# Diagonal inverses in a half-width tile copied by ScalarE, two key fetches moved back, and other ranks for the woven jobs

## The chip, the cores and the metric

One core of one Trainium2 chip. The metric is the device time of one execution in microseconds (us); each run gives one such time. The engines are TensorE (PE in the profile; PEld are its weight loads), VectorE (DVE), ScalarE (ACT), GpSimd (POOL) and SyncE (SP), whose queue issues every DMA of this kernel.

## The reference, cut to what matters

A decoder step of two layers over 1024 prompt tokens and 8 x 4 sample tokens, width 1024. Layer 0 is sliding-window attention (16 query heads on 4 key heads), in which the sample tokens also see 128 cached keys and values. Layer 1 is gated DeltaNet: 16 value heads on 8 key heads, in chunks of 64 tokens, each of which needs the inverse of a unit lower triangular matrix.

```
def swa_sample_core(q, k, v, k_buf, v_buf, sinks):
    k_all = jnp.concatenate([k_buf.astype(k.dtype), k], axis=1)
...
    p = sink_softmax(logits, mask, sinks)
...
def gated_delta_chunked(q, k, v, g, beta, s0, chunk):
...
    lower = jnp.where(strict, jnp.einsum('nbhik,nbhjk->nbhij', kb, kc) * decay, 0.0)
    rhs = jnp.concatenate([vc * bc[..., None], kb * jnp.exp(gc)[..., None]], axis=-1)
    sol = lax.linalg.triangular_solve(lower + jnp.eye(chunk, dtype=lower.dtype), rhs,
                                      left_side=True, lower=True, unit_diagonal=True)
...
    def step(S, xs):
        w_v_c, w_k_c, qk_c, q_dec_c, k_dec_c, g_tot_c = xs
        u = w_v_c - jnp.einsum('bhck,bhkv->bhcv', w_k_c, S)
        o = jnp.einsum('bhck,bhkv->bhcv', q_dec_c, S) + jnp.einsum('bhij,bhjv->bhiv', qk_c, u)
        S = S * g_tot_c[..., None, None] + jnp.einsum('bhck,bhcv->bhkv', k_dec_c, u)
        return S, o
```

## The kernel before

Every projection runs on TensorE in split precision: weights and activations are cut into a high and a low part (`wh` and `wl`, `hhi` and `hlo`), and each of the 8 steps over the 1024 inputs is three matmuls, high by high, low by high and high by low. The tokens are taken in three groups of 384, 384 and 288 columns. The kernel is one chain of such projection matmuls; everything else is a set of Python generators, the jobs, whose instructions are put between them.

The order is fixed while the program is built. Between two projection matmuls `stages()` goes through the jobs in the order of their ranks (`K` by name of job, `KT` for the closing, `KR` by DeltaNet round) and lets each run that is not held back. A job holds itself with `ready` (its tile is done by a planner's clock), `soon` and `idle` (done, or its engine free, within a margin: `AM` in the layers, `AT` in the closing), or waits for a PSUM `bank`. The planner (`class Core`) gives each issued instruction a cost and a due time. So a new number in these tables, or another cost, moves instructions of all engines from there to the end; each engine then runs its own list strictly in order.

The stages, by time in the profile: a head written out by hand (0 to 50 us); attention (50 to 390), near whose end `cached` treats the sample tokens in four pairs; the projection `wo` back to the model width (390 to 500); DeltaNet in 8 rounds, one for each key head (500 to 1340); the output projection of DeltaNet, woven with the last rounds' state chain and the sample states (the closing, 1340 to 1590); a tail.

`cached` fetches for each pair `KT` and `vc` from the caches by `cached_rows` and a mask `smk`. `cached_pair` scores them into a PSUM bank (`kxs,qz` and `KT,qz`), takes the softmax on VectorE and ScalarE (`sp`, `smx`, `snm`, `es`, `ssu`), turns it on TensorE (`erl,sp`; `erl` holds the identity) and multiplies by the values (`spT,vc`). `load_wo` fetches the weights of `wo` (`wor`, `wr`), ScalarE rounds them to `whi`, and VectorE or GpSimd, by `GP[0]`, takes the rest `wlo`.

In a DeltaNet round `solve` builds the triangular matrices `UZ` and stores their 32 x 32 diagonal blocks in DRAM (`Ld`). `invert` loads them as `X`, 64 blocks at a time on 2 x 64 partitions, and solves for the inverse with 31 pairs of VectorE operations; it stores the result to `Xdd` and loads it back turned, as `Xc`. `diagonal` writes `Xc` into the block-diagonal tile `Xd`, which TensorE multiplies with `UZ` (`Xd,UZ`), and `blocks` combines the pieces (`UZ,M`). `chain` is the recurrence over the chunks: `S,kT` gives `vo`, `vo,UZ` gives `uo` (copied by ScalarE), `uo,ks` updates the state `S` on VectorE, and `S,qT` and `uo,DP` give the output.

Nearly all operations are recorded at the helper's line L84 (L83 after the change), so that the tiles tell them apart.

Of the kernel before, what the change touches and what calls it, by code (L numbers as in the profile page):

```python
# [5 lines left out]
F32 = mybir.dt.float32  # L6
# [25 lines left out]
def constants():  # L32
# [29 lines left out]
    blocks["fold32"] = (i[:, None] % 32 == np.arange(32)[None, :]) * 1.0  # L62
    order = ["ident", "fold32", "iu", "ones", "mku", "lo32", "bsel", "fold64", "wmask", "smask", "selp", "sels"]
    blocks = {k: blocks[k] for k in order}
# [29 lines left out]
class Core:  # L94
# [15 lines left out]
    def issued(self, eng, op, ins, args, kwargs):  # L110
# [18 lines left out]
        if "dma" in op:  # L129
# [168 lines left out]
def body(tc, I, O, cst_ap, dbg=None):  # L298
# [19 lines left out]
    SP = (2, 20)  # L318
    AM = (3, 12)
    AT = (-5, 3)  # L320
    EX = (1.2, 1.6, 0, 0.9)
    ES, EN, EL, EM = EX
    K = {'split': 12, 'add': 26, 'attend': 22, 'turning': 24, 'modulate': 20, 'cached': 8, 'wo': 60, 'turn': 0, 'ahead': 2, 'taps': 2, 'gating': 6, 'decay': 23, 'samples': 28, 'load': 6, 'mod': 1, 'shape': 27, 'decays': 35, 'prepare': 61, 'gather': 23, 'finish': 37, 'states': 7, 'core': 16, 'new': 8}
    KT = {'prepare': 3, 'gather': 15, 'finish': 25, 'states': 10, 'core': 7, 'new': 9, 'load': 12, 'gating': 5, 'samples': 30, 'output': 24}
    KR = [{'chain': 4, 'output': 20, 'solve': 6, 'invert': 19, 'blocks': 31, 'decayed': 22}, {'chain': 31, 'output': 29, 'solve': 13, 'invert': 31, 'blocks': 39, 'decayed': 38}, {'chain': 31, 'output': 2, 'solve': 30, 'invert': 41, 'blocks': 2, 'decayed': 6}, {'chain': 35, 'output': 37, 'solve': 4, 'invert': 4, 'blocks': 10, 'decayed': 23}, {'chain': 14, 'output': 0, 'solve': 23, 'invert': 44, 'blocks': 1, 'decayed': 57}, {'chain': 41, 'output': 36, 'solve': 8, 'invert': 4, 'blocks': 58, 'decayed': 16}, {'chain': 8, 'output': 15, 'solve': 8, 'invert': 12, 'blocks': 57, 'decayed': 12}, {'chain': 10, 'output': 18, 'solve': 42, 'invert': 34, 'blocks': 0, 'decayed': 60}]
    TB = (3, 5)
    SW = (16, 13)
    MS = (50, 5)
# [3 lines left out]
    MM = (11, 12)  # L332
    ORDER = [("q", 2), ("q", 3), ("q", 4), ("q", 5), ("z", 0), ("k", 1), ("z", 1), ("z", 2), ("q", 6), ("q", 7),
# [242 lines left out]
    def ready(*ts):  # L576
        return lambda: plain() or nc.ready(ts) <= nc.free["tensor"]
# [433 lines left out]
    if True:  # L1011
# [869 lines left out]
    if True:  # L1881
# [155 lines left out]
        def solve(hq, st):  # L2037
# [21 lines left out]
            Ld = dr.tile([64, 32, 32], F32, name="Ld", tag="Ld", bufs=2)  # L2059
            Xdd = dr.tile([2, 64, 32, 32], F32, name="Xdd", tag="Xdd", bufs=2)  # L2060
            UZ = st["UZ"] = []
# [25 lines left out]
        def invert(hq, st, Ld, Xdd):  # L2087
# [6 lines left out]
            for p in range(2):  # L2094
                nc.sync.dma_start(X[64 * p:64 * p + 64], Ld)
            yield soon(X)
            for p in range(2):
                nc.gpsimd.memset(X[64 * p:64 * p + 64].rearrange("p i c -> p (i c)")[:, 32 * p:1024:65], 1.0)
            nc.gpsimd.memset(X[64:P, 0, 0:1], 0.0)
            yield soon(X)  # L2100
            for k in range(31):
                n, m = 31 - k, k // 2 + 1
                tv = tmp[:, 0:n * m].rearrange("p (i c) -> p i c", c=m)
                yield idle("vector")
                nc.vector.tensor_tensor(tv, X[:, k, k + 1:].unsqueeze(2).to_broadcast([P, n, m]),
                                        X[:, k, 0:m].unsqueeze(1).to_broadcast([P, n, m]), ALU.mult)
                nc.vector.tensor_tensor(X[:, k + 1:, 0:m], X[:, k + 1:, 0:m], tv, ALU.subtract)
            nc.sync.dma_start(Xdd.rearrange("p q i c -> (p q) i c"), X)
            inverted[0] += 1
            yield lambda: solved[0] == hq  # L2110
            Xc = gs.tile([P, 16, 2, 16], F32, tag="Xc", name="Xc")
            for b in range(4):
                for p in range(2):
                    nc.sync.dma_start(Xc[32 * b:32 * b + 32, :, p, :],
                                      Xdd[p, 16 * b:16 * b + 16, :, 0:16].rearrange("q i c -> i q c"))

            lg, Ms, uzs = "lg", [], [t_.rearrange("p h c i -> p (h c) i") for t_ in UZ]

            def diagonal():

                for cp_, uz in enumerate(uzs):
                    xd = Xd[cp_ % 2]
                    yield soon(Xc)
                    for b in range(4):
                        bs = slice(32 * b, 32 * b + 32)
                        nc.gpsimd.tensor_tensor(xd[bs, :, bs].rearrange("i q (c p) -> i q p c", p=2), Xc[bs, 4 * cp_:4 * cp_ + 4],
                                                C["lo32"][bs, :].rearrange("i (p c) -> i p c", p=2).unsqueeze(1)
                                                .to_broadcast([32, 4, 2, 16]), ALU.mult)
                    yield lambda: st.get("pairs", 0) >= cp_ - 2
                    yield ready(xd)  # L2130
# [933 lines left out]
```

## Time and profile before

| | |
|---|---|
| time, median of 3 runs | 1600.68 us (1599.53 to 1602.54) |
| the profiled execution's own time | 1600.59 us |
| its span | 1598.8 us |
| its mean granted TensorE clock | 0.997 |
| TensorE busy | 1573.9 us, 98% |
| VectorE busy | 1215.9 us, 76% |
| ScalarE busy | 843.0 us, 53% |
| GpSimd busy | 145.1 us, 9% |

The span is the time from the first to the last instruction that the profiler records; 1.8 us of the execution's time lie outside it. Busy shares are means over stages.

### The profile page before, as it was taken

How to read it: one execution, taken by the hardware profiler on the slowest of the kernel's cores; microseconds unless marked ns; L12 is line 12 of the kernel's file. 1: busy time of each engine (PE TensorE's matmuls, PEld its weight loads, DVE VectorE, ACT ScalarE, POOL GpSimd, SP SyncE). 2: the span in 40 equal slices, each digit the busy share in tenths (PEclk: the TensorE clock that was granted, in tenths of full speed). 3: DMA queues.
4: the chain of work that ended last, by engine and by line, in shares of the span. 5: the costliest groups of instructions: out<-in, count | busy, mean ns of one | idle time of the engine just before them, and what ended most of it. 6: DMA issues, size and time to landing. Idle time of an engine off the chain costs nothing. (4 is left out here: it accounts for less than half of the span.)

```text
span 1598.8 us, 30691 instructions
## 1 busy us (share of the span) xinstructions
PE 1573.9 (98%) x10714; PEld 1404.9 (88%) x10714; DVE 1215.9 (76%) x3830; ACT 843.0 (53%) x2422; POOL 145.1 (9%) x231
## 2 busy tenths in 40 slices
PE   9999999999999999999999999999999999999997
PEld 6888888988778999999999999999999998767776
DVE  5737667676676678987988778888688887858787
ACT  4635655554344665565564655755557565523332
POOL 1300000000001002020020100202001002121121
PEclk9999999999999999999999999999999999999999
DMA  9542220106252333143433325323243136685874
GB/s 366 157 142 80 80 82 27 40 25 194 89 171 87 90 95 76 55 124 88 120 73 86 100 56 131 86 56 110 75 117 92 49 92 217 204 270 184 272 278 162
DMA packets 178572, 195.71 MB, mean 122 GB/s; under 512 B 76593, under 2 KB 120465, under 8 KB 178385
## 3 DMA queue, kind: packets, MB, share of 16 engines
q1 hardware_dynamic: 178416, 193.75, 40.0%
q8 instruction: 85, 1.39, 0.4%
q14 instruction: 71, 0.57, 0.1%
HBM read 146.45 MB, written 49.27 MB: 122 GB/s over the span
## 5 line engine op out<-in xcount | busy, mean ns | idle before, releaser
L84 PE MATMUL ps_pj<-h2hi,wh 128*128 128x384 f32 (+1 forms) x1128 | 378.1, 335 | 0.0
L84 PE MATMUL ps_pj<-h2hi,wl 128*128 128x384 f32 (+1 forms) x1128 | 377.1, 334 | 0.2 <-DVE wl L84 0.2
L84 PE MATMUL ps_pj<-h2lo,wh 128*128 128x384 f32 (+1 forms) x1128 | 376.9, 334 | 0.0
L84 PEld LDWEIGHTS ps_pj<-h2hi,wl 128*128 128x128 f32 x1128 | 213.1, 189 | 2.4 <-DVE wl L84 0.5
L84 PEld LDWEIGHTS ps_pj<-h2lo,wh 128*128 128x128 f32 x1128 | 213.3, 189 | 2.2
L84 PEld LDWEIGHTS ps_pj<-h2hi,wh 128*128 128x128 f32 x1128 | 213.2, 189 | 2.0
L84 PE MATMUL ps_pj<-hhi,wh 128*128 128x384 f32 (+1 forms) x376 | 123.8, 332 | 0.5 <-ACT hhi L84 0.4
L84 PE MATMUL ps_pj<-hlo,wh 128*128 128x384 f32 (+1 forms) x376 | 122.8, 330 | 0.0
L84 PE MATMUL ps_pj<-hhi,wl 128*128 128x384 f32 (+1 forms) x376 | 122.3, 329 | 0.0
L84 POOL TENSOR_TENSOR Xd<-Xc,cst 32x128 f32<-32x128 f32 x128 | 67.1, 524 | 456.5 <-DMA Xc<-Xdd 307.2
L84 DVE SCALAR_TENSOR_TENSOR vT<-XR,cT,vT 128x384 f32<-128x384 f32 (+1 forms) x144 | 82.6, 579 | 16.8 <-ACT vT L84 15.0
L84 DVE TENSOR_TENSOR wl<-wr,wh 128x512 fp32r<-128x512 f32 x120 | 82.9, 691 | 10.6 <-ACT wh L84 9.9
L84 ACT CAST wh<-wr 128x512 fp32r<-128x512 f32 x128 | 78.6, 616 | 18.7 <-PE ps_pj L84 17.9
L84 PEld LDWEIGHTS ps_pj<-hlo,wh 128*128 128x128 f32 x376 | 70.6, 188 | 8.2 <-issue 7.7
L84 PEld LDWEIGHTS ps_pj<-hhi,wh 128*128 128x128 f32 x376 | 70.5, 188 | 6.6 <-issue 4.8
L84 ACT COPY XR<-ps_pj 128x384 f32<-128x384 f32 (+1 forms) x96 | 43.6, 454 | 57.4 <-PE ps_pj L84 57.0
L84 PEld LDWEIGHTS ps_pj<-hhi,wl 128*128 128x128 f32 x376 | 70.6, 188 | 3.7 <-issue 3.7
L84 ACT ACTIVATE prob<-prob,nm 128x256 f32<-128x256 f32 (+1 forms) x128 | 62.3, 489 | 18.9 <-DVE nm L84 18.8
L84 DVE TENSOR_TENSOR X<-X,tmp 128x126 f32<-128x126 f32 (+22 forms) x248 | 63.8, 257 | 8.5
L84 DVE TENSOR_TENSOR tmp<-X 128x126 f32<-128x126 f32 (+22 forms) x248 | 62.4, 252 | 8.2 <-POOL X L84 3.6
L84 ACT ACTIVATE qe<-ps_mi,Eg 128x128 f32<-128x128 f32 x112 | 35.0, 364 | 63.0 <-PE ps_mi L84 59.8
L84 POOL TENSOR_TENSOR xt<-xt,y 128x512 f32<-128x512 f32 x30 | 42.5, 1419 | 182.9 <-DVE y L84 166.9
(555 smaller groups left out, 3824.5 us busy)
## 6 DMA issues: line engine op xcount, KB each, us to landing
wr<-in_gwb SPq DMA_DIRECT2D x96, 256.0 KB
S<-in_states SPq DMA_DIRECT2D x42, 256.0 KB
wm<-in_wm SPq DMA_DIRECT2D x16, 512.0 KB
wr<-in_winb SPq DMA_DIRECT2D x32, 256.0 KB
wmod<-in_w_mod SPq DMA_DIRECT2D x32, 256.0 KB
wm<-in_w_mod SPq DMA_DIRECT2D x32, 256.0 KB
DP<-gcr SPq DMA_DIRECT2D x64, 128.0 KB
zl<-zd SPq DMA_DIRECT2D x32, 256.0 KB
```

The lines of the kernel that those rows point to most:

```text
L84: inst = fn(*args, **kwargs)
```

## The change

It has six parts.

1. `invert` solves into a clean tile `Y` of 16 columns, which GpSimd clears and gives its unit diagonal, where the inverse was written over the lower half of `X`; `Xdd` has half the size.
2. In `diagonal`, `Xd` is written by 128 ScalarE copies where it was 128 GpSimd multiplications with the mask `lo32`. The copies wait for `idle("scalar", Xc)` each, and the wait for `pairs` stands ahead of them.
3. `cached_pair` fetches pairs 2 and 3 only when the pair before has its keys (`looked`).
4. `gct` lies in another pool, and the unread output of `turn_sum` is one shared tile `jk`.
5. The planner takes a load to 64 partitions as 0.8 longer.
6. `GP[0]` is 1: the second half of each of the 8 rows of `wlo` goes to GpSimd. The other tables get new numbers, of which a few lines stand below (`EX`, `KT`, `KR`, `TB`, `SW`, `MS` and `MM` change in the same manner).

```diff
@@ -132,6 +131,8 @@
             self.moved = max(start + 0.7, self.moved) + 2.4 * size + 0.0005 * rows
             end = self.moved + self.dl[0 if outs[0].space == DRAM else 1]
+            if outs[0].space != DRAM and outs[0].shape[0] == 64:
+                end += 0.8
...
@@ -316,20 +317,20 @@
-    AM = (3, 12)
-    AT = (-5, 3)
+    AM = (2, 14)
+    AT = (-6, 7)
...
-    GP = (0, 0, 0, 0, 1)
-    ORD = ['zzkv', 'zqvzk', 'zqzkv', 'qzzvk', 'qzzkv', 'vqzzk', 'qzzkv', 'qvzz']
+    GP = (1, 0, 0, 0, 1)
+    ORD = ['zzkv', 'zqvzk', 'zqvzk', 'zqzkv', 'qzzkv', 'vqzzk', 'qzzkv', 'qvzz']
...
@@ -1326,10 +1327,11 @@
-            yield lambda: paired[0] >= b2 - 2
+            yield lambda: paired[0] >= b2 - 2 and (b2 < 2 or looked[0] >= b2 - 1)
             KT, vc = held[b2] if b2 < 2 else cached_rows(b2)
             yield lambda: paired[0] >= b2 - 1
             yield ready(KT)
+            looked[0] += 1
...
@@ -2093,26 +2096,26 @@
-            yield soon(X)
+            Y = gs.tile([P, 32, 16], F32, tag="Y", name="Y")
+            nc.gpsimd.memset(Y, 0.0)
             for p in range(2):
-                nc.gpsimd.memset(X[64 * p:64 * p + 64].rearrange("p i c -> p (i c)")[:, 32 * p:1024:65], 1.0)
-            nc.gpsimd.memset(X[64:P, 0, 0:1], 0.0)
-            yield soon(X)
+                nc.gpsimd.memset(Y[64 * p:64 * p + 64].rearrange("p i c -> p (i c)")[:, 16 * p:512:33], 1.0)
+            yield soon(X, Y)
...
-                                        X[:, k, 0:m].unsqueeze(1).to_broadcast([P, n, m]), ALU.mult)
-                nc.vector.tensor_tensor(X[:, k + 1:, 0:m], X[:, k + 1:, 0:m], tv, ALU.subtract)
-            nc.sync.dma_start(Xdd.rearrange("p q i c -> (p q) i c"), X)
+                                        Y[:, k, 0:m].unsqueeze(1).to_broadcast([P, n, m]), ALU.mult)
+                nc.vector.tensor_tensor(Y[:, k + 1:, 0:m], Y[:, k + 1:, 0:m], tv, ALU.subtract)
+            nc.sync.dma_start(Xdd.rearrange("p q i c -> (p q) i c"), Y)
...
@@ -2120,13 +2123,11 @@
-                    yield soon(Xc)
+                    yield lambda: st.get("pairs", 0) >= cp_ - 2
                     for b in range(4):
                         bs = slice(32 * b, 32 * b + 32)
-                        nc.gpsimd.tensor_tensor(xd[bs, :, bs].rearrange("i q (c p) -> i q p c", p=2), Xc[bs, 4 * cp_:4 * cp_ + 4],
-                                                C["lo32"][bs, :].rearrange("i (p c) -> i p c", p=2).unsqueeze(1)
-                                                .to_broadcast([32, 4, 2, 16]), ALU.mult)
-                    yield lambda: st.get("pairs", 0) >= cp_ - 2
+                        yield idle("scalar", Xc)
+                        nc.scalar.copy(xd[bs, :, bs].rearrange("i q (c p) -> i q p c", p=2), Xc[bs, 4 * cp_:4 * cp_ + 4])
```

What this moves is seen in the lists of the engines, of which three places stand here. The number of built matmuls is the same before and after, 9022; the groups in which they are not projection matmuls are 560 before and 555 after.

**The cached pairs.** TensorE, end of the attention layer, before; `...` stands for projection matmuls (`ps_pj`) alone:

```order
L84 MATMUL ps_lg<-kxs,qz 32x32 x8
L84 MATMUL ps_lg<-KT,qz 32x128 x8
L84 MATMUL ps_pj<-hlo,wh 128x384
...
L84 MATMUL ps_lg<-kxs,qz 32x32 x8
L84 MATMUL ps_lg<-KT,qz 32x128 x8
...
L84 MATMUL ps_pj<-hhi,wh 128x288
L84 MATMUL ps_mi<-erl,sp 128x128
L84 MATMUL ps_mi<-erl,sp 32x128
```

and after the change:

```order
L83 MATMUL ps_lg<-kxs,qz 32x32 x8
L83 MATMUL ps_lg<-KT,qz 32x128 x8
...
L83 MATMUL ps_lg<-kxs,qz 32x32 x8
L83 MATMUL ps_lg<-KT,qz 32x128 x8
...
L83 MATMUL ps_mi<-erl,sp 128x128
L83 MATMUL ps_mi<-erl,sp 32x128
L83 MATMUL ps_pj<-hlo,wh 128x384
L83 MATMUL ps_mi<-erl,sp 128x128
L83 MATMUL ps_mi<-erl,sp 32x128
L83 MATMUL ps_pj<-hhi,wl 128x384
```

Before, 21 projection matmuls (5 of 288 columns, 16 of 384) stand between the last attention block's `ob<-pT,vsb` and the first of these groups, 5 between the two groups, and 28 from the second group to the first `erl,sp`; the second pair's `erl,sp` comes far behind. After, they are 26 (18 of 288, 8 of 384), 6 and 14, and the second pair's `erl,sp` follows one matmul behind the first's.

SP's queue at that place, before and then after; `in_wob` are the weights of `wo`:

```order
L84 DMA wr<-in_wob 128x512 x2
L84 DMA KT<-in_keysT 64x1024
L84 DMA vc<-in_cache_swa_v 128x2x256
...
L84 DMA smk<-in_cst 128x640
L84 DMA KT<-in_keysT 64x1024
L84 DMA vc<-in_cache_swa_v 128x2x256
L84 DMA wor<-in_wob 128x512 x4
```

```order
L83 DMA wr<-in_wob 128x512
L83 DMA KT<-in_keysT 64x1024
L83 DMA vc<-in_cache_swa_v 128x2x256
...
L83 DMA smk<-in_cst 128x640
L83 DMA wor<-in_wob 128x512 x3
L83 DMA KT<-in_keysT 64x1024
L83 DMA vc<-in_cache_swa_v 128x2x256
```

One `wr` fewer stands ahead of the first keys, and the third pair's keys stand behind three `wor`. VectorE runs, before, the first softmax through to its end and then the second; after, both are interleaved: `sp`, `smx`, `snm`, `es` of the one and of the other, then the two sums and divisions.

**GpSimd's list**, from the `wo` weights to the second DeltaNet round, before:

```order
L84 MEMSET spT 128x128 x4
L84 TENSOR_TENSOR kw0l<-wr,kw0h 128x512
...
L84 MEMSET X 64x16 x2
L84 MEMSET X 64x1
L84 TENSOR_TENSOR Xd_6460<-Xc,cst 32x4x2x16 x4
L84 TENSOR_TENSOR Xd_6462<-Xc,cst 32x4x2x16 x4
```

and after:

```order
L83 TENSOR_TENSOR wlo<-wor,whi 128x512
L83 MEMSET spT 128x128 x2
L83 TENSOR_TENSOR wlo<-wor,whi 128x512 x3
...
L83 TENSOR_TENSOR wlo<-wr,whi 128x512 x4
L83 TENSOR_TENSOR kw0l<-wr,kw0h 128x512
...
L83 MEMSET Y 128x512
L83 MEMSET Y 64x16 x2
```

Eight subtractions `wlo` have come to GpSimd, and in each of the 8 rounds 16 multiplications into `Xd` have gone, for one full and two strided memsets of `Y`; ScalarE's list has 16 copies into `Xd` more in each round.

**The state chain of the last round**, on TensorE in the closing, before:

```order
L84 MATMUL ps_pj<-h2lo,ohi 128x512
L84 MATMUL ps_ob<-vo,UZ 128x128 x2
L84 MATMUL ps_mi<-uo,ks 128x128 x2
L84 MATMUL ps_mi<-S,qT 128x256
L84 MATMUL ps_mi<-uo,DP 128x128 x2
L84 MATMUL ps_pj<-h2hi,ohi 128x512
```

and the tightest place after:

```order
L83 MATMUL ps_mi<-uo,ks 128x128 x2
L83 MATMUL ps_mi<-S,qT 128x256
L83 MATMUL ps_mi<-uo,DP 128x128 x2
L83 MATMUL ps_mi<-S,kT 128x256
L83 MATMUL ps_tr<-erl,vo 128x128 x8
L83 MATMUL ps_ob<-vo,UZ 128x128 x2
L83 MATMUL ps_pj<-h2hi,ohi 128x512
L83 MATMUL ps_pj<-h2hi,of 128x512
L83 MATMUL ps_mi<-uo,ks 128x128 x2
```

Before, `uo,ks` follows `vo,UZ` with nothing between them at one place and with one matmul at another; after, at least two projection matmuls stand between them everywhere. In turn `S,kT` now follows `uo,DP` at once at one place, with `erl,vo` alone between it and `vo,UZ`.

## Rows read from the trace of the kernel before

**Rows 1.** The page: span, and busy time of each engine.

```profile
span 1598.8 us, 30691 instructions
PE 1573.9 (98%) x10714; PEld 1404.9 (88%) x10714; DVE 1215.9 (76%) x3830; ACT 843.0 (53%) x2422; POOL 145.1 (9%) x231
```

**Rows 2.** Windows: stretch, us, busy PE, PEld, DVE, ACT, POOL; clock, DMA share, GB/s.

```profile
357.00:370.00 13.00, 11.80 (x123) 10.70 (x123) 4.47 (x18) 3.00 (x9) 0.35 (x2) 1.00 0.96 257
500.00:1340.00 840.00, 837.28 (x6107) 804.41 (x6106) 688.06 (x2182) 496.33 (x1461) 74.65 (x161) 1.00 0.34 90
1340.00:1500.00 160.00, 153.51 (x812) 112.65 (x811) 120.04 (x323) 66.58 (x163) 23.30 (x21) 1.00 0.73 231
```

**Rows 3.** Waits of TensorE, 1340 to 1500: releaser, total, times, longest.

```profile
PE ps_pj L84 <- DVE y L84: 1.1, 1, 1.1
...
PE ps_mi L84 <- DVE S L84: 0.7, 1, 0.7
```

**Rows 4.** Timeline of TensorE: start, duration, operation; an attention visit.

```profile
348.41 0.34 PE L84 MATMUL ps_pj<-hhi,wl 128*128 128x384 f32 x1
348.58 0.34 PE L84 MATMUL ps_pj<-hhi,wh 128*128 128x384 f32 x1
348.76 1.04 PE L84 MATMUL ps_mi<-erl,prob 128*128 128x128 f32 x8
349.55 0.42 PE L84 MATMUL ps_pj<-hlo,wh 128*128 128x384 f32 x1
```

**Rows 5.** Timeline of the cached pairs, all engines; in brackets the idle time before.

```profile
340.73 15.86 SPq L84 DMA_DIRECT2D wr<-in_wob  x2
...
361.93 0.64 PE L84 MATMUL ps_lg<-KT,qz 64*32 64x128 f32 x16 [1.16 <-DMA vc<-in_cache_swa_v]
...
365.91 0.32 DVE L84 CUSTOM_DVE_ANT_0 sp<-ps_lg,smk 128x160 f32<-128x160 f32 x1 [6.16 <-DMA smk<-in_cst]
...
368.15 0.56 DVE L84 SCALAR_TENSOR_TENSOR zo<-th,zo 128x384 f32<-128x384 f32 x1
...
369.01 0.30 DVE L84 TENSOR_SCALAR sp<-sp,ssu 128x160 f32<-128x160 f32 x1
...
369.49 0.38 PE L84 MATMUL ps_mi<-erl,sp 128*128 128x128 f32 x2
```

**Rows 6.** Timeline of the closing's state chain; then the group of all `olo`.

```profile
1354.81 0.71 PE L84 MATMUL ps_mi<-uo,ks 128*128 128x128 f32 x4 [0.52 <-ACT uo L84]
...
1361.18 1.28 POOL L84 TENSOR_TENSOR xt<-xt,y 128x512 f32<-128x512 f32 x1 [15.85 <-DVE y L84]
1361.22 1.79 DVE L84 TENSOR_TENSOR olo<-of,ohi 128x512 fp32r<-128x512 f32 x1
...
1365.63 0.67 PE L84 MATMUL ps_mi<-S,kT 128*128 128x256 f32 x2 [0.70 <-DVE S L84]
L84 DVE TENSOR_TENSOR olo<-of,ohi 128x512 fp32r<-128x512 f32 x30 | 22.5, 754 | 15.2 <-ACT ohi L84 15.0
```

**Rows 7.** By tile `Xd`: durations in ns, min/median/max; GpSimd's waits; then two ScalarE groups.

```profile
L84 POOL TENSOR_TENSOR Xd<-Xc,cst x128: 442/455/1004, 624.3 to 1328.0; 32x128 f32<-32x128 f32 x128
L84 POOL MEMSET Xd<- x2: 528/528/529, 549.8 to 550.2; 128x512 f32 x2
...
  DMA Xc<-Xdd: 307.2, 24
...
L84 ACT ACTIVATE vo<-vo,fo 128x128 f32<-128x128 f32 x128 | 41.5, 394 | 9.9 <-DVE fo L84 9.9
L84 ACT ACTIVATE jk<-ps_lg 128x128 f32<-128x128 f32 x120 | 33.5, 279 | 14.5 <-PE ps_lg L84 11.8
```

**Rows 8.** Timeline: last `wlo` on VectorE, its use on TensorE, a GpSimd subtraction.

```profile
395.26 1.90 DVE L84 TENSOR_TENSOR wlo<-wr,whi 128x512 fp32r<-128x512 f32 x3 [1.14 <-ACT whi L84]
...
401.50 0.39 PE L84 MATMUL ps_mi<-wlo,ohi 128*128 128x512 f32 x1
...
493.97 1.36 POOL L84 TENSOR_TENSOR kw0l<-wr,kw0h 128x512 fp32r<-128x512 f32 x1 [116.37 <-DMA xt<-in_x_prompt]
```

More of the change, by code (lines that the diff above doesn't have):

```diff
@@ L62, in constants @@
     blocks["fold32"] = (i[:, None] % 32 == np.arange(32)[None, :]) * 1.0
-    order = ["ident", "fold32", "iu", "ones", "mku", "lo32", "bsel", "fold64", "wmask", "smask", "selp", "sels"]
+    order = ["ident", "fold32", "iu", "ones", "mku", "bsel", "fold64", "wmask", "smask", "selp", "sels"]
     blocks = {k: blocks[k] for k in order}
@@ L318, in body @@
     SP = (2, 20)
-    AM = (3, 12)
-    AT = (-5, 3)
-    EX = (1.2, 1.6, 0, 0.9)
+    AM = (2, 14)
+    AT = (-6, 7)
+    EX = (0.7, 1.6, 0, 0.9)
     ES, EN, EL, EM = EX
-    K = {'split': 12, 'add': 26, 'attend': 22, 'turning': 24, 'modulate': 20, 'cached': 8, 'wo': 60, 'turn': 0, 'ahead': 2, 'taps': 2, 'gating': 6, 'decay': 23, 'samples': 28, 'load': 6, 'mod': 1, 'shape': 27, 'decays': 35, 'prepare': 61, 'gather': 23, 'finish': 37, 'states': 7, 'core': 16, 'new': 8}
-    KT = {'prepare': 3, 'gather': 15, 'finish': 25, 'states': 10, 'core': 7, 'new': 9, 'load': 12, 'gating': 5, 'samples': 30, 'output': 24}
@@ L326, in body @@
-    TB = (3, 5)
-    SW = (16, 13)
-    MS = (50, 5)
+    K = {'split': 16, 'add': 11, 'attend': 22, 'turning': 24, 'modulate': 5, 'cached': 33, 'wo': 60, 'turn': 0, 'ahead': 2, 'taps': 2, 'gating': 6, 'decay': 22, 'samples': 52, 'load': 6, 'mod': 1, 'shape': 27, 'decays': 35, 'prepare': 31, 'gather': 40, 'finish': 58, 'states': 4, 'core': 1, 'new': 37}
+    KT = {'prepare': 3, 'gather': 35, 'finish': 38, 'states': 10, 'core': 7, 'new': 11, 'load': 12, 'gating': 5, 'samples': 37, 'output': 32}
@@ L329, in body @@
+    TB = (3, 6)
+    SW = (1, 22)
+    MS = (51, 9)
     AH, AI = (a / 10 for a in AM)
-    GP = (0, 0, 0, 0, 1)
-    ORD = ['zzkv', 'zqvzk', 'zqzkv', 'qzzvk', 'qzzkv', 'vqzzk', 'qzzkv', 'qvzz']
-    MM = (11, 12)
+    GP = (1, 0, 0, 0, 1)
+    ORD = ['zzkv', 'zqvzk', 'zqvzk', 'zqzkv', 'qzzkv', 'vqzzk', 'qzzkv', 'qvzz']
+    MM = (11, 18)
     ORDER = [("q", 2), ("q", 3), ("q", 4), ("q", 5), ("z", 0), ("k", 1), ("z", 1), ("z", 2), ("q", 6), ("q", 7),
@@ L1834, in decays @@
         yield soon(p2)
+        gct = ab.tile([P, P], F32, name="gct")
         nc.scalar.copy(gct, p2[:, 0:P])
@@ L1858, in decays @@
             nc.gpsimd.memset(Xd[i], 0.0)
+        junk.append(gs.tile([P, P], F32, name="jk"))
         weave(decay_blocks(0, states[0]), "decay")
@@ L2023, in turn_sum @@
                     nc.tensor.transpose(pt[:, c * P:(c + 1) * P], src[:, cc * P:(cc + 1) * P], ident)
-                jk = gs.tile([P, P], F32, tag="jk" if ktok is None else "jn", name="jk")
+                jk = junk[0]
                 for c in range(4):
@@ L2059, in solve @@
             Ld = dr.tile([64, 32, 32], F32, name="Ld", tag="Ld", bufs=2)
-            Xdd = dr.tile([2, 64, 32, 32], F32, name="Xdd", tag="Xdd", bufs=2)
+            Xdd = dr.tile([2, 64, 32, 16], F32, name="Xdd", tag="Xdd", bufs=2)
             UZ = st["UZ"] = []
@@ L2114, in invert @@
                     nc.sync.dma_start(Xc[32 * b:32 * b + 32, :, p, :],
-                                      Xdd[p, 16 * b:16 * b + 16, :, 0:16].rearrange("q i c -> i q c"))
+                                      Xdd[p, 16 * b:16 * b + 16].rearrange("q i c -> i q c"))
             lg, Ms, uzs = "lg", [], [t_.rearrange("p h c i -> p (h c) i") for t_ in UZ]
```

6 lines of the change are left out of this document (2 added, 4 removed).

## The prediction

> **What bounds the kernel now.** The page comes first [rows 1]: TensorE is busy for 1573.9 of 1598.8 us, VectorE for 76%, ScalarE for 53%, GpSimd for 9%. So time can be gained only where TensorE stands still, 24.9 us in all, or by fewer or cheaper matmuls. The windows by stage come next, since a mean over stages hides where that is [rows 2]: in DeltaNet, 840 us long, TensorE lacks 840 - 837.28 = 2.7 us; in the closing 160 - 153.51 = 6.5 us; in the 13 us around the cached pairs 1.2 us. That is 10.4 of the 24.9; the rest is the head, which the change leaves alone, and the tail behind the last matmul. The waits of TensorE in the closing are several of about a microsecond, each with a releaser of its own (the residual sum `y` 1.1, the state `S` 0.7) [rows 3]. The granted clock is 1.00 in all these windows, so there is none to win. The reader is to see: whatever work the change takes from GpSimd, VectorE or ScalarE counts only as far as it shortens one of these waits. The sum is made against the profiled execution's 1600.59 us, 0.09 below the median of the runs.
>
> **Matmuls and their groups.** The built matmuls are as many as before. Five groups of other matmuls between the projection ones are gone. What a visit costs beyond its own matmuls is seen at one in attention [rows 4]: projection matmuls start 0.17 us apart, and the first behind the visit takes 0.42 in place of 0.34, so 0.08. Five fewer give -0.4; the ends are 0, if the visit costs nothing, and -0.8, at twice the row.
>
> **The cached pairs.** Now TensorE waits 1.16 us for the first pair's loads, at 361.93, and reaches the first `erl,sp` at 369.49, just behind the division that ended at 369.01 + 0.30 = 369.31 [rows 5]. That softmax began at 365.91, when the mask `smk` landed (6.16 us idle, released by its DMA), and took 3.4 us, of which VectorE spent the time up to 368.71 on other work, `zo` last.
>
> After the change, 26 projection matmuls stand ahead of the first keys' scores where 21 did. At 0.174 us for 384 columns and, in proportion, 0.13 for 288, that is 8 x 0.174 + 18 x 0.13 = 3.7 us against 16 x 0.174 + 5 x 0.13 = 3.4: TensorE arrives 0.3 later, so the wait for loads is 0.85 if they land as now. From there to the first `erl,sp` stand 6 + 14 = 20 matmuls where 5 + 28 = 33 did, 13 x 0.174 = 2.3 us less: TensorE gets there at about 367.2 on the clock of now. The softmax is shorter too, since nothing but the second pair's first half lies in it: from 3.4 us take off `th` and `zo`, 2 x 0.56 = 1.1, leaving 2.3, so 365.9 + 2.3 = 368.2. If `smk` lands as now, TensorE waits 1.0 us there and about 0.2 at the second pair, one matmul later: 0.85 + 1.2 = 2.05 against 1.16, a loss of 0.9. But one `wr` of 256 KB fewer stands ahead in the queue, whose stage moves 257 GB/s at a DMA share of 0.96 [rows 2]; that is 1.0 us. If all lands so much earlier, the wait for the loads is gone and the one for `sp` is about 0.9 in all (the start moves ahead with the loads): a gain of 0.3. I take the middle, +0.3. The ends: -1.2, if nothing is left of any wait, and +3, if the softmax takes its 3.4 us as now and the second pair adds 0.7. Pairs 2 and 3 are fetched later, behind three or six `wor`; their scores come some 20 matmuls (3.5 us) or more behind, and the row's DMA share says that the queue is full, so that is part of the +3.
>
> **The closing.** `uo,ks` waited 0.52 us for ScalarE's `uo` where nothing stood between it and `vo,UZ` [rows 6]; now at least two matmuls of 0.23 us stand there, so -0.5. In turn `S,kT` comes right behind `uo,DP` at one place, with eight `erl,vo` (8 x 0.11 = 0.9 us, the visit of [rows 4] gives 0.79 + 0.08 for eight) between it and `vo,UZ`. VectorE must make two `vo` from it meanwhile; I put that at some 1.3 us, as two operations of the size of `S` (0.60 for two) behind the matmul's own 0.67. So +0.4. The 5.5 us that are left of closing waits come from bad meetings, such as this one: `olo` took 1.79 us where the mean of 30 is 0.754, beside a GpSimd addition of 1.28 us that began 0.04 us earlier, and `S`, behind it on VectorE, then cost TensorE 0.70 [rows 6]. All ranks and margins there are new; some meetings go and others come. I take -1.0. The ends: -5.5, all gone, and +4, if the new order keeps the old waits and adds more than half as many.
>
> **`Xd` from GpSimd to ScalarE.** 128 GpSimd operations of 524 ns (67 us) go [rows 7]; GpSimd had 307 us of idle time for `Xc` to spare, and TensorE never waited for it. ScalarE gets 128 copies. Their price is not in the trace; from below it is nothing, if they lie in its idle time, from above 394 ns, a 128 x 128 operation out of on-chip memory; the nearest is 279 ns, one of 128 columns. I take 0.30, 38 us in all. In DeltaNet ScalarE is busy for 496 of 840 us, 59% [rows 2]; 64% then, and still no wall. What is behind a copy that must wait for `Xc` is another matter: ScalarE takes its list in order, so `M`, `uo` and `qe` stand behind it. In the changed order the copies of a round stand behind the store of `Xdd` by 36 to 60 projection matmuls, 6 to 10 us at 0.17 [rows 4], and the store moves half the bytes, so they should find `Xc` landed. The eight full memsets of `Y` (528 ns each) are GpSimd's and fall in the time of the load of `X`. VectorE's 31 pairs of operations keep their sizes. Taken together -0.3 (ends -2.7, the stage's whole waits, and +2).
>
> **`wlo` on GpSimd.** A GpSimd subtraction takes 1.36 us, VectorE's 0.63. The last three `wlo` end at 397.16 on VectorE, and TensorE uses the first of the last four second halves at 401.50 [rows 8]: 4 us of cover over a loss of 0.7. So 0. Were that cover gone, the price would be 0.7 for each of four.
> The rows of `olo` show what else such work can do: two engines at once, one of them blocked for the other's whole length. The Trainium skill has this as a rule ("SBUF — State Buffer", section "Who interferes with whom"): a VectorE operation with two inputs in on-chip memory contends with a GpSimd one that reads there, and the second blocks until the first is done. The trace agrees (1.79 against 0.754). By it each of the eight could put 1.3 us on VectorE, and the 128 that leave DeltaNet would give VectorE time back; neither is on TensorE's path by the rows of that stage.
>
> **The sum.** -0.4 + 0.3 - 0.5 + 0.4 - 1.0 - 0.3 = -1.5: 1600.6 - 1.5 = 1599.1 us, 0.1% below. A measurement of this kernel tells about 0.2% (3.2 us) from no change, so this is no change.
>
> **The rivals.**
> *The closing's waits go.* For it: they are single meetings, and nearly every job's rank is new, so few will meet again. Against: each is released by another engine, so no one cause can go. With -5 there and the other terms as above, 1595. Chance 0.33.
> *The cached pairs' softmax becomes the wait.* TensorE comes 2.3 us earlier to `erl,sp`. If the mask lands no earlier and the two softmaxes run as slowly as the one now, +3, and with the third pair's later keys, which stand behind 6 x 256 KB (6 us at 257 GB/s), another 1.5. It decides when TensorE stands for more than about 5 us in all there: 1600.6 + 4.5 - 1.2 = 1604. For it: the DMA share of 0.96. Against: three stages of order between those keys and their use. Chance 0.12.
> *ScalarE stands for `Xc`.* If copies come to the head of its list before `Xc` has landed, `M` and `uo` are late in each of 8 rounds, 0.6 us each time: +5, 1604 to 1606. It decides from some 4 us of waiting, as two projection groups' banks of 24 x 0.174 us lie between. Against: the 6 to 10 us above. Chance 0.07.
> *VectorE blocked by GpSimd in `wo`.* If each of the eight blocks a VectorE operation as `olo` was blocked (1.79 - 0.75 = 1.0 us), 8 us fall on VectorE, half of them on the last four, against 4 of cover: +2 at most, 1601, which is still no change. Chance 0.05.
> The forecast, no change, has 0.43 beside this last.
>
> **Range and chances.** Faster by over 0.2% 0.33; within 0.48; slower 0.19. The likeliest case's own range is 1597.5 to 1603.9. For 8 in 10 I reach into both sides: 1593 (the closing's -5.5 with the ends of the groups and DeltaNet) to 1605.
>
> **What would show it.** Right: TensorE's busy time within 1 us of 1573.9; no GpSimd `Xd`, ScalarE near 880 us busy; a wait of TensorE at `erl,sp` of 0.5 to 1.5 us, and less than 1.2 for the first keys; no wait for `uo` in the closing, and one of some 0.4 for `vo` there. Wrong: a ScalarE wait for `Xc` with TensorE idle behind it; closing waits under 2 us or over 9; any stage whose TensorE idle time moves by more than 3 us.

## The result, and the profile after

The changed kernel takes 1607.67 us (median of 7 runs, 1604.09 to 1609.74) against 1600.64 us before (7 runs, 1599.16 to 1602.54): 1.0041 times as long, 95% interval 1.0029 to 1.0053. It is slower by 0.4%, where no change was forecast. The profiled execution took 1608.17 us.

The page of the changed kernel, span and busy times, to be set beside [rows 1]:

```profile
span 1606.4 us, 30656 instructions
PE 1577.7 (98%) x10714; PEld 1405.4 (87%) x10714; DVE 1203.5 (75%) x3822; ACT 879.7 (55%) x2550; POOL 94.7 (6%) x111
```

The work moved as the diff says: GpSimd has 50 us less, ScalarE 37 more. TensorE is busy 3.8 us longer and stands still 28.7 us in place of 24.9. The windows of the changed kernel, in the columns of [rows 2], say where:

```profile
357.00:370.00 13.00, 12.36 (x127) 10.76 (x126) 7.02 (x25) 5.24 (x17) 1.65 (x3) 1.00 0.87 246
500.00:1340.00 840.00, 833.44 (x6045) 800.62 (x6043) 673.47 (x2171) 529.21 (x1580) 11.53 (x33) 1.00 0.32 86
1340.00:1500.00 160.00, 154.83 (x857) 114.66 (x856) 121.69 (x325) 68.41 (x169) 22.67 (x20) 0.98 0.72 228
```

In DeltaNet TensorE lacks 6.6 us where it lacked 2.7; around the cached pairs 0.6 where it lacked 1.2. In the closing up to 1500 us it lacks 5.2 where it lacked 6.5, but the clock of that window is 0.98, and up to 1590 us it lacks 7.1 where it lacked 7.0. So the added idle time lies in DeltaNet. The longest of its waits there, and then the two longest up to 1500 us (releaser, total, times, longest), are

```profile
PE ps_ob L83 <- DVE UZ L83: 3.6, 5, 1.2
...
PE ps_tr L83 <- DVE zl L83: 1.7, 1, 1.7
PE ps_mi L83 <- DVE S L83: 1.4, 1, 1.4
```

The first are five places where `vo,UZ` stands for a `UZ` that VectorE has not made yet; the kernel before has no such wait. The last two lie one behind the other at the place that stood last in the order of the state chain: `S,kT` at once behind `uo,DP`. The timeline of the changed kernel there:

```profile
1368.04 0.68 DVE L83 TENSOR_TENSOR y<-ps_pj,gp 128x512 f32<-128x512 f32 x1
1368.64 0.60 DVE L83 SCALAR_TENSOR_TENSOR S<-S,Gt,ps_mi 128x128 f32<-128x128 f32 x2
1368.95 1.27 POOL L83 TENSOR_TENSOR xt<-xt,y 128x512 f32<-128x512 f32 x1 [140.00 <-DMA raw<-cvd]
1369.16 2.14 DVE L83 TENSOR_SCALAR ks<-ktok,sd 128x128 f32<-128x128 f32 x1
1369.39 0.67 PE L83 MATMUL ps_mi<-S,kT 128*128 128x256 f32 x2 [1.37 <-DVE S L83]
...
1370.15 1.06 POOL L83 MEMSET zq<- 128x256 f32 x4
...
1371.29 0.73 DVE L83 SCALAR_TENSOR_TENSOR zl<-ps_tr,ong,zl 128x512 f32<-128x512 f32 x1
...
1372.16 1.08 PE L83 MATMUL ps_tr<-erl,vo 128*128 128x128 f32 x4 [1.67 <-DVE zl L83]
```

VectorE takes `y` before `S`, so `S,kT` waits. Then `ks`, an operation of 0.28 us, takes 2.14: it ends just behind GpSimd's addition and the four memsets, and `zl` and TensorE wait behind it. TensorE has then stood still for most of four microseconds, and its clock falls, from 1.00 to 0.50, that is from 2.4 to 1.2 GHz, from 1371.3 to 1378.1. Three of the windows of 1 us (clock third from the end):

```profile
1370.00:1371.00 1.00, 0.49 (x5) 0.25 (x3) 1.00 (x3) 1.00 (x4) 1.00 (x5) 1.00 0.77 240
1372.00:1373.00 1.00, 0.84 (x4) 0.87 (x5) 1.00 (x5) 0.00 (x0) 0.00 (x0) 0.50 0.15 53
1375.00:1376.00 1.00, 1.00 (x5) 0.97 (x5) 0.12 (x1) 0.61 (x2) 0.00 (x0) 0.50 0.74 248
```

Those 6.8 us at half speed cost at most 3.4 us. The kernel before had one such stretch too, 3.4 us long from 531.8, by its windows of 1 us, and there TensorE had not stood still: it was busy for all of the 6 us ahead, with 18 matmuls of 32 columns among the last. Its timeline, in which a matmul then takes 0.52 in place of 0.34:

```profile
529.10 2.14 PE L84 MATMUL ps_lg<-erl,abT 64*128 64x32 f32 x18
...
531.45 0.34 PE L84 MATMUL ps_pj<-h2hi,wh 128*128 128x384 f32 x1
...
531.80 0.52 PE L84 MATMUL ps_pj<-h2hi,wl 128*128 128x384 f32 x1
```

### The profile page after: what moved, and what is told of

Its sections match the earlier page's. It is cut to its first block, busy times and chain, and to the rows that moved or that the text cites. A ratio compares the mean times of both kernels' runs of the same rounds, so it can differ in the third digit from the quotient of the medians.

```text
span 1606.4 us, 30656 instructions
## 1 busy us (share of the span) xinstructions
PE 1577.7 (98%) x10714; PEld 1405.4 (87%) x10714; DVE 1203.5 (75%) x3822; ACT 879.7 (55%) x2550; POOL 94.7 (6%) x111
## 5 line engine op out<-in xcount | busy, mean ns | idle before, releaser
L83 DVE TENSOR_TENSOR Y<-Y,tmp 128x126 f32<-128x126 f32 (+22 forms) x248 | 63.7, 257 | 9.0
L83 DVE TENSOR_TENSOR tmp<-X,Y 128x126 f32<-128x126 f32 (+22 forms) x248 | 62.6, 252 | 4.8
L83 ACT COPY uo<-ps_ob 128x256 f32<-128x256 f32 x64 | 23.6, 369 | 74.1 <-PE ps_ob L83 73.9
```

The source lines that it names most:

```text
L83: inst = fn(*args, **kwargs)
```

## The experiments

All times are medians; each ratio is to runs of the kernel before on the same chip, with its 95% interval, and these ratios are what is compared. Most experiments keep an order: an instruction is run by another engine while the planner counts it for the old one, so that TensorE's list stays word for word. The form of that edit, `nc.issued(engine for the planner, operation, real instruction, operands)`, is the planner's own entry.

| run | us | ratio | interval |
|---|---|---|---|
| the change | 1607.67 | 1.0041 | 1.0029 to 1.0053 |
| tables | 1629.98 | 1.0166 | 1.0153 to 1.0180 |
| code | 1627.87 | 1.0155 | 1.0136 to 1.0175 |
| plan_only | 1614.19 | 1.0077 | 1.0065 to 1.0089 |
| pool_xd | 1604.69 | 1.0018 | 1.0009 to 1.0026 |
| code_pool_xd | 1618.36 | 1.0108 | 1.0091 to 1.0125 |
| act_only | 1614.63 | 1.0085 | 1.0070 to 1.0100 |
| act_twice | 1625.65 | 1.0153 | 1.0135 to 1.0172 |
| filler | 1606.68 | 1.0030 | 1.0018 to 1.0041 |
| spread | 1613.77 | 1.0072 | 1.0060 to 1.0085 |
| pool_xd_unblk | 1602.60 | 1.0009 | 0.9997 to 1.0020 |
| wlo_raw | 1606.21 | 1.0029 | 1.0019 to 1.0040 |
| three | 1603.52 | 1.0005 | 0.9996 to 1.0014 |
| pool_nomask | 1599.42 | 0.9984 | 0.9973 to 0.9995 |
| y_pool | 1599.59 | 0.9981 | 0.9971 to 0.9990 |
| y_pool_unblk | 1597.32 | 0.9966 | 0.9954 to 0.9978 |

### Tables and code apart

The first theory (A) was the meeting in the closing, its rivals that the code edits cost (B), above all ScalarE's copies, and that any new order is a new draw of meetings (C).

`tables`: the kernel before with the twelve tables of the change.

> The kernel before with all rank and margin tables of the change (AM, AT, EX, K, KT, KR, TB, SW, MS, GP, ORD, MM) and none of its code edits. Theory A (the loss is made by the new order: in the closing two waits of 1.37 and 1.67 us one behind the other, then 6.8 us at the lower clock): as slow as the change, 1604 to 1609 us, if this order holds the same meeting. Rival B (the loss is made by the code edits, ScalarE's copies into Xd making UZ late in DeltaNet): 1599 to 1602 us. Rival C (any new order is a new draw of meetings): anything from 1597 to 1608, with waits at places that neither kernel has.

`code`: the changed kernel with the twelve tables of before.

> The changed kernel with all tables of the kernel before: the code edits alone (Y, ScalarE's copies, later fetch of the cached pairs, gct and jk moved, 0.8 in the planner). Theory A: 1599 to 1602 us, no stretch at the lower clock in the closing. Rival B: about 2 us over the kernel before from DeltaNet alone, 1602 to 1604, with TensorE waits for UZ of 3 us or more there. Rival C: as above.

Neither came near its range: 1630 and 1628 us. Each half alone loses four times what both together lose. In `tables` the longest wait of TensorE in DeltaNet is for `vT`, in `code` for ScalarE's `Xd` (releaser, total, times, longest):

```profile
PE ps_tr L84 <- ACT vT L84: 5.0, 2, 4.2
```

```profile
PE ps_lg L83 <- ACT Xd L83: 3.2, 2, 1.8
```

So the tables belong to the code: with the code edits in place the new tables gain 1.1%, some 18 us, over the old ones. What a new order alone can cost is shown by the smallest edit that makes one.

```diff
             end = self.moved + self.dl[0 if outs[0].space == DRAM else 1]
+            if outs[0].space != DRAM and outs[0].shape[0] == 64:
+                end += 0.8
```

> The kernel before with one edit of the change, the planner's 0.8 us for loads to 64 partitions: no instruction more or less, but a new order from the first such load on. Theory C: a new draw of meetings, 1603 to 1625 us, since the old tables fit the old order alone. If the order matters little: 1599 to 1602.

1614.2 us: the planner's 0.8, not one instruction more or less, costs 0.8% under the old tables, as C had it. That is one draw of an order, not a fixed price. Its window of DeltaNet shows 840 - 825.27 = 14.7 us without work on TensorE:

```profile
500.00:1340.00 840.00, 825.27 (x5934) 791.77 (x5933) 675.74 (x2151) 491.08 (x1447) 69.54 (x155) 1.00 0.32 87
```

and its waits there are many and mostly small:

```profile
PE ps_mi L84 <- ACT uo L84: 3.0, 6, 0.5
PE ps_pj L84 <- DVE wl L84: 2.8, 3, 2.2
```

### ScalarE's copies

```diff
-                        nc.scalar.copy(xo_, xi_)
+                        nc.issued("scalar", "copy", nc.nc.gpsimd.tensor_copy(xo_, xi_).ins, (xo_, xi_), {})
```

(`xo_` and `xi_` are the operands of the copy into `Xd`.) In the changed kernel:

> The changed kernel with the 128 copies into Xd run by GpSimd, while the planner still counts them as ScalarE's, so that the order on TensorE, VectorE and SP stays as it is word for word. Theory B (ScalarE's copies hold up what stands behind them and make UZ late): DeltaNet's waits for UZ go and the time falls by 2 to 4 us, to 1603 to 1606. Theory C (the new order itself holds the bad meetings, whoever copies): within 2 us of the changed kernel, 1606 to 1609.

In `code`:

> The kernel of the run with the code edits under the old tables (1628 us), with its copies into Xd run by GpSimd as above, its order on TensorE kept. Theory B: the waits of TensorE for Xd (3.2 us) and UZ go, and the time falls to 1610 to 1616. Theory C: 1624 to 1630.

1604.7 us is in the range of B; 1618.4 lies between the two ranges. The copies cost the changed kernel 0.23% (1.0041 to 1.0018) and the old tables 0.47%, with every list but ScalarE's and GpSimd's as it was. GpSimd makes such a copy as fast as ScalarE, as the tile `Xd` of `pool_xd` shows (durations in ns, min/median/max); ScalarE's in the changed kernel have 282/303/315:

```profile
L2131 POOL COPY Xd<-Xc x128: 282/294/759, 615.0 to 1329.1; 32x128 f32<-32x128 f32 x128
```

and in its window of DeltaNet TensorE lacks 4.9 us in place of 6.6:

```profile
500.00:1340.00 840.00, 835.14 (x6072) 803.25 (x6071) 677.40 (x2173) 493.24 (x1459) 58.78 (x161) 1.00 0.32 86
```

The five waits for `UZ` are still there (3.5 us), though B had them go; what went are five of 0.2 to 0.3 us, and one of 0.6 at 542 us, ahead of the first copy into `Xd` at 616. So the traces place about 1 us of the 0.23% (3 to 4 us); where the rest lies is not shown, and the trace of `pool_xd` is also without the half-speed stretch in the closing. ScalarE does stand for `Xc` in the changed kernel:

```profile
ACT Xd L83 <- DMA Xc<-Xdd: 5.8, 9, 0.9
```

Within 5 us behind these waits TensorE is seen to wait for ScalarE only once, 0.2 us for `M`, so they hardly reach it. The opposite edit puts the copies on ScalarE in the old order:

```diff
-                        nc.gpsimd.tensor_tensor(xo_, xi_, lo_, ALU.mult)
+                        nc.issued("gpsimd", "tensor_tensor", nc.nc.scalar.copy(xo_, xi_).ins, (xo_, xi_, lo_), {})
```

> The kernel before with its 128 multiplications into Xd replaced by ScalarE's copies, which the planner still counts as GpSimd's, so that the order on TensorE, VectorE and SP is that of before word for word. The mask on the 32 x 32 blocks is left out. Theory B: slower by 5 us or more, 1606 to 1620, with ScalarE waiting for Xc. Theory C: 1599 to 1603, as the copies alone cost nothing where the order stays.

1614.6 us, 0.85% slower, as B had it: the copies alone, 38 us of work on an engine that was 59% busy, put 10 us more of idle time on TensorE in DeltaNet. The window of DeltaNet:

```profile
500.00:1340.00 840.00, 827.08 (x5964) 792.98 (x5964) 668.47 (x2154) 528.02 (x1577) 7.48 (x33) 1.00 0.32 87
```

The first of TensorE's waits in it:

```profile
PE ps_lg L84 <- ACT Xd L2128: 4.8, 4, 2.8
```

And the timeline of the longest of these, ScalarE's rows with TensorE's at the end:

```profile
1232.84 0.31 ACT L2128 COPY Xd<-Xc 32x128 f32<-32x128 f32 x1
...
1233.70 1.28 ACT L84 ACT_TABLE_LOAD   x1
1234.99 2.19 ACT L84 ACTIVATE DP<-DP 128x512 f32<-128x512 f32 x4
1237.19 1.28 ACT L84 ACT_TABLE_LOAD   x1
...
1239.03 0.62 ACT L2128 COPY Xd<-Xc 32x128 f32<-32x128 f32 x2
...
1239.38 1.13 PE L84 MATMUL ps_lg<-Xd,UZ 128*128 128x96 f32 x8 [2.76 <-ACT Xd L2128]
```

Two of the four pieces of an `Xd` are made by 1233.2; the other two stand behind the exponentials of the decay blocks and their two table loads, 4.8 us in a row, and TensorE waits for the fourth. No idle time stands ahead of these two copies, so here it is the list that kept them, not the landing of `Xc`. (B expected ScalarE to wait for `Xc`; it does so four times in this trace, 2.9 us in all.) GpSimd's list, in the kernel before, had nothing but such pieces there.

`act_twice` makes each copy of the changed kernel twice:

```diff
+                        i_ = nc.nc.scalar.copy(xo_, xi_).ins
                         nc.scalar.copy(xo_, xi_)
```

> The changed kernel with each of ScalarE's 128 copies into Xd made twice, the planner counting one; TensorE's and VectorE's order stay. If the copies cost by their place in ScalarE's list (B): at least the 3 us again that GpSimd's copies gave back, 1611 to 1620 us. If ScalarE has room for them, as was predicted: 1607 to 1609.

1625.7 us, beyond the range of B. The second 38 us cost 18 where the first cost 3 or 4. That the new tables had found an order in which most of the copies fit, with no room for more, would explain it, but is not shown. TensorE waits nine times for `Xd` in it:

```profile
PE ps_lg L83 <- ACT Xd L83: 4.4, 9, 1.0
```

### The meeting in the closing

`filler` keeps TensorE at work there, with matmuls that nobody reads: three by the lines below ahead of `S,kT`, and four by a like loop in `gating`, ahead of the second `erl,vo`.

```diff
+                        spin.append(lambda: nc.nc.tensor.matmul(py[:, 256:512], kT[:, 0:P], kT[:, 0:256], start=True, stop=True))
+                        for _ in range(3):
+                            spin[0]()
```

> The changed kernel with seven more matmuls of 256 columns (0.43 us each), whose results nobody reads, at the one place of the closing where TensorE waits for S and for zl: four ahead of S,kT and three between the two groups of erl,vo. The rest of the order stays. Theory A: TensorE no longer stands still there, the clock stays at 2.4 GHz, and though work is added the time falls by about 3 us, to 1603 to 1605 us. If the clock falls for another reason: it falls again, and the time stays at 1606 to 1609 us.

1606.7 us, a ratio of 1.0030: the direction is that of A, but the time lies in the range of the other case, and the interval meets that of the change, so a gain is not shown. In TensorE's list four of them came ahead of `S,kT` and three behind. The timeline of TensorE shows that they fill the gap, and the clock stays at 1.00 there, as it does in `pool_xd` with the gap open:

```profile
1368.76 1.89 PE L2292 MATMUL ps_ob<-kT 128*128 128x256 f32 x8
...
1371.36 1.46 PE L2292 MATMUL ps_ob<-kT 128*128 128x256 f32 x6
1373.07 0.63 PE L83 MATMUL ps_tr<-erl,vo 128*128 128x128 f32 x4 [0.25 <-DVE zl L83]
```

But the next thing that was late came to the front: the wait for `kb` grew from 0.7 to 2.7 us, and behind it, from 1517.5 to 1521.0, lies a stretch at 0.50.

`spread` puts projection matmuls there instead, by two lines in `chain` that hold `S,kT` and `vo,UZ` of chunk 5 back by two steps each; the order behind them follows anew.

> The changed kernel with two steps of the output projection (six matmuls) put ahead of the one S,kT that follows uo,DP at once, and two ahead of the vo,UZ behind it; the order behind that place follows anew. Theory A: neither wait nor the stretch at the lower clock: 1600 to 1603 us. If the place is not the cause: 1606 to 1609 us.

1613.8 us, outside both ranges and slower than the change. The wait for `S` at the place is gone, that for `zl` is down to 0.3, and elsewhere in the closing there are new ones, as C has it:

```profile
PE ps_pj L83 <- DVE ohi L83: 4.3, 1, 4.3
PE ps_pj L83 <- DVE y L83: 2.8, 1, 2.8
```

So the place had to be mended without moving anything. `pool_xd_unblk` is `pool_xd` with one addition on VectorE:

```diff
+            if n == 0:
+                i_ = nc.nc.vector.tensor_tensor(xt[:, ns], xt[:, ns], y, ALU.add)
+                nc.issued("gpsimd", "tensor_tensor", i_.ins, (xt[:, ns], xt[:, ns], y), {})
+            else:
+                getattr(nc, eng).tensor_tensor(xt[:, ns], xt[:, ns], y, ALU.add)
```

> The changed kernel with its copies into Xd on GpSimd (1604.7 us) and, besides, the closing's first addition into xt on VectorE (0.68 us) where GpSimd made it (1.27 us); the order of TensorE, ScalarE and SP stays. If that addition, and the four memsets behind it, are what keeps VectorE's ks at 2.15 us in place of 0.28: ks falls under 0.5 us, TensorE's wait for zl (1.7 us) falls under 0.6, and the time falls by 1 to 2 us, to 1603. If VectorE is only busy there: no change, 1604 to 1605.5.

1602.6 us, ratio 1.0009; the interval meets that of `pool_xd` (1.0018), so the gain of 0.1% is not clear of the noise. `ks` is back at 0.28 us, though VectorE does more. The four memsets are gone from beside it too: GpSimd makes them at 1346.6, some 20 us earlier, so the run does not tell them from the addition.

```profile
1366.56 0.69 DVE L2527 TENSOR_TENSOR xt<-xt,y 128x512 f32<-128x512 f32 x1
...
1367.16 0.28 DVE L83 TENSOR_SCALAR ks<-ktok,sd 128x128 f32<-128x128 f32 x1
...
1369.05 0.63 PE L83 MATMUL ps_tr<-erl,vo 128*128 128x128 f32 x4 [1.15 <-DVE zl L83]
```

The wait for `zl` fell from 1.7 to 1.15, not under 0.6, as the addition itself now takes 0.69 of VectorE.

### `wlo`, and all three together

`wlo_raw` is the changed kernel with all `wlo` on VectorE, by the same kind of edit.

> The changed kernel with the eight wlo of GpSimd made by VectorE, the planner counting them as GpSimd's; TensorE's order stays. As predicted (hidden by some 4 us of cover): no difference, 1606 to 1609 us. If GpSimd's wlo block VectorE on the path: 1 to 2 us faster, 1605.5 to 1606.5.

1606.2 us, 1.0029, a time in both ranges; the intervals meet, so a gain is not shown, and the window from 390 to 500 us is full in both (110.00 of 110). `three` takes back all three:

> The changed kernel with three things at once, TensorE's order kept: copies into Xd on GpSimd, the closing's first addition into xt on VectorE, all wlo on VectorE. If the loss of the change is the sum of ScalarE's copies (3.0 us), GpSimd's addition in the closing (2.1) and at most 1.5 for wlo: 1601 to 1602.6 us, level with the kernel before. If something else in the new order costs: over 1604.

1603.5 us, 1.0005 (0.9996 to 1.0014): level with the kernel before. The time was 0.9 over the expected span, the ratio is what was expected. That does not yet mean that the new order is as good as the old one, since `three` has the first edit of the change and the kernel before has not; the next runs tell them apart.

### The first edit in the old order

`pool_nomask` is the kernel before with GpSimd copying where it multiplied (the edit of `act_only`, with `nc.nc.gpsimd.tensor_copy`).

> The kernel before with its 128 multiplications into Xd replaced by GpSimd copies from Xc alone, the planner counting multiplications; all orders stay. The mask on the 32 x 32 blocks is left out. If the mask's second input costs (524 ns in the mean, or VectorE blocked beside it): 1 to 2 us faster, 1599.5 to 1600.5. If it is hidden: 1601 to 1602.5.

1599.4 us, faster by 0.16%. Beside `act_only` (1.0085), which leaves out the mask alike and differs in the copying engine alone, ScalarE in GpSimd's place costs 1.0% in the old order. Without a mask the blocks above the diagonal must be zero, which is what the clean tile `Y` gives. `y_pool` has `Y`, the half-size `Xdd` and the moved `gct` and `jk`; every planner entry is made for the old operands, and its lists of TensorE and ScalarE are those of before.

> The kernel before with the change's first edit alone (the inverse in a clean tile Y, half-size Xdd, gct and jk moved to make room) and Xd copied from Xc by GpSimd without a mask; the planner counts as before, so that TensorE's and ScalarE's orders are those of before word for word. If the mask's multiplication was what cost: 1599 to 1600 us, the 0.16% of the run without a mask, now with the reference's outputs. If Y's memset or its loads cost: 1601 to 1603.

1599.6 us, 0.9981: the first edit of the change, with GpSimd's plain copies, is a gain, as large as that of leaving out the mask alone. With the closing's first addition on VectorE as above:

> The same with the closing's first addition into xt on VectorE in place of GpSimd, beside which olo took 1.79 us before. If that meeting cost TensorE its wait for S (0.7 us): another 0.5 to 1 us off, 1598 to 1599.5. If not: as the run without it.

1597.3 us, 0.9966 (0.9954 to 0.9978), below the expected range and faster than both kernels. Its `olo`, which took 1.79 us beside GpSimd's addition [rows 6], takes 0.69, and the wait for `S` is gone from its list; in the trace of `y_pool` they were 1.51 and 0.4. How much this second step gains is less clear, as the intervals of the two runs meet. In its windows TensorE lacks 2.9 us in DeltaNet and 4.6 in the closing (6.5 before, 4.4 in the trace of `y_pool`):

```profile
500.00:1340.00 840.00, 837.10 (x6120) 804.83 (x6119) 684.57 (x2187) 497.20 (x1464) 58.80 (x169) 1.00 0.33 88
1340.00:1500.00 160.00, 155.41 (x822) 114.66 (x821) 119.27 (x324) 67.44 (x166) 24.61 (x21) 1.00 0.72 234
```

This run and `three` (1603.52 us on the same chip) settle what the new order is worth. Both have the tile `Y`, GpSimd's copies, the first addition and all `wlo` on VectorE, and by their traces they run the same instructions, but for eight small memsets; what differs is the order, the later key fetches among it. The new one is slower by 0.39%, 6 us. In DeltaNet `three` lacks 5.5 us where this run lacks 2.9, and the five waits for `UZ` are in `three` alone. Its window of DeltaNet and its longest wait there:

```profile
500.00:1340.00 840.00, 834.46 (x6080) 802.32 (x6078) 678.69 (x2175) 493.65 (x1459) 59.12 (x161) 1.00 0.32 86
...
PE ps_ob L83 <- DVE UZ L83: 3.5, 5, 1.1
```

## Why the prediction was wrong, point by point

**What bounds the kernel.** Right: what the traces place of the loss is TensorE standing still or at half clock. What followed from it was not: that some 10 us of waits are all that can be gained says nothing of what can be lost. The order before is one in which the engines' lists meet well: `plan_only` leaves it at a cost of 12 us with no work changed, and the order of the change is 0.39%, 6 us, slower with the same work. The sum put a new order at a gain alone, the -1.0 of the closing, and at nothing in DeltaNet.

**Groups of matmuls.** -0.4 cannot be seen; TensorE's busy time rose by 3.8 us, where it was to stay within 1; the stretch at half clock is part of that.

**The cached pairs.** +0.3 was expected, with 1.2 us of waiting for `sp`. The loads landed earlier, as the better of the two cases had it; the timeline of the changed kernel has a wait of 0.58 for the second pair's keys and none for the first's:

```profile
363.50 0.64 PE L83 MATMUL ps_lg<-KT,qz 64*32 64x128 f32 x16 [0.58 <-DMA KT<-in_keysT]
...
366.84 0.16 PEld L83 LDWEIGHTS ps_mi<-erl,sp 128*128 128x128 f32 x2 [0.38 <-DVE sp L83]
```

The softmax took 2.0 us (364.82 to 366.79) against the 2.3 worked out, and the window lost 0.6 us of idle time. So in this window the step was right in kind and 0.9 us too dear; over the whole of attention, from 50 to 390 us, TensorE lacks 2.4 us where it lacked 2.5, which is next to nothing gained.

**The closing.** The place was named, and -0.5, +0.4 and -1.0 put on it. `vo` did wait (0.7 where 0.4 was expected), and `uo` fell only from 0.5 to 0.3. What failed is that only `vo` was priced at the tight place: `S,kT` behind `uo,DP` also waits for `S` (1.37), which VectorE makes behind `y`, and VectorE itself was blocked by GpSimd for two microseconds, as `olo` had been. The row of that blocking was read [rows 6] and used for the old meeting alone, not for the question whether GpSimd's next addition would meet something worse. By the medians it cost some 0.1% (1.0018 to 1.0009, with intervals that meet), besides the stretch at half clock, which is in some traces only. The -1.1 us of these three terms came out as 0.1 us more idle time from 1340 to 1590 us.

**`Xd` from GpSimd to ScalarE.** This is the step that failed: the term for DeltaNet, with the overlap of ScalarE's copies in it. It was put at -0.3 with +2 as its dear end, and TensorE's idle time there rose by 3.9 us (2.7 to 6.6), past the 3 us that the prediction itself had named as a sign of being wrong. The copies measured 0.23%, 3 to 4 us, in the new order and 0.85%, 13 us, in the old one; the five late `UZ`, 3.5 us, come with the new order and stay when the copies go. The price of a copy was right (0.30 expected, 303 ns), the share too (59% to 63%), and copies wait for `Xc` 9 times in 128. Wrong was what was looked for: what stands behind a copy, not what stands ahead of it. ScalarE's list is in order, and it holds blocks of 4.8 us (two table loads around exponentials) that GpSimd's did not. That this is the cost is shown in the old order; in the new one TensorE's own waits for `Xd` are 0.2 us. A share of 63% is no measure of the room; `act_twice` shows how fast it runs out.

**`wlo`.** Not told from zero, as expected.

**The rivals.** The cached pairs' softmax did not become the wait. "ScalarE stands for `Xc`", at a chance of 0.07, was the nearest: ScalarE does stand, for 5.8 us in all, but TensorE is hardly seen to wait behind it, and the time of 1604 to 1606 was still too low. The rival that was missing is the plainest: a new order can be slower than the one that it replaces. By the ratios, the steps from `y_pool_unblk` (0.9966) to the changed kernel (1.0041) are +0.39% for the new order with the same work, +0.04% for `wlo` on GpSimd (not told from zero), +0.09% for the addition on GpSimd (not clear of the noise) and +0.23% for ScalarE's copies. So the gain of the first edit was there, and hidden by the rest. Two of the prediction's sums are also off, with nothing resting on them: the 1604 of the softmax rival takes the other terms as -1.2, and they add up to -1.8, which gives 1603.3; the lower end of 1593 comes out at 1591.8 by the ends that it names.

**Open.** Why TensorE's clock falls at the meeting in one execution and not in another: `pool_xd` has the same two waits (1.37 and 1.69 us) and stays at 1.00, and in the kernel before the clock fell where TensorE had no wait. The Trainium skill ("TensorE: Matmul & The Clock Gate", section "Part 1: The HAM clock gate (the "warmup" mystery)") says that a monitor sets the clock by how busy the engine has been, and that its phase differs from run to run. The two traces of the meeting do not speak against that, none shows the phase, and the fall in the kernel before came with TensorE busy in the profile's sense. How much of the spread of the changed kernel's runs, 1604.1 to 1609.7, comes from it was not measured; the shortest had a mean clock of 0.999 and the longest of 0.995. Open too is what makes `UZ` late in the new order, and where most of the 0.23% of ScalarE's copies lies there.

## What to carry to other kernels

An order that a planner or a search has fitted is part of the kernel's speed: price any edit that redraws it by what a redrawn order has cost (0.8% in one draw here, 0.39% in the order of the change), and try an edit first with the order held, where it shows its own worth. Before moving work to an engine with room on average, read that engine's list ahead of the place where the work must stand, and look for its longest block. A good part can hide in a bad whole: of this change, the clean tile with plain GpSimd copies gains 0.2% in the old order.

## What the runs showed of the hardware that was not expected

A VectorE `TENSOR_SCALAR` of 128 x 128, 0.28 us by itself, took 2.14 us while GpSimd made an addition of 1.27 us and then four memsets of 1.06 us, and ended 0.09 us behind them; with the addition on VectorE and the memsets 20 us earlier it took 0.28. The Trainium skill ("SBUF — State Buffer", section "Who interferes with whom") has `tensor_scalar` among the operations that can contend with GpSimd for the shared ports; the trace agrees, without telling the addition's part from that of the memsets. GpSimd's plain copy of a 32 x 128 block took 294 ns in the median and its multiplication by a mask 455 [rows 7]; ScalarE's copy took 303.
